# Attention's blocks counted and paced over the slabs, the product operands formed in the last slab, and two of W_o's weights in the values' buffers

## The chip, the cores and the metric

The kernel runs on one core of a Trainium2 chip. The metric is the device time of one execution in microseconds (us); lower is better. Five engines run their own instruction streams side by side: TensorE (PE, matrix products and transposes into PSUM), VectorE (DVE), ScalarE (ACT), GpSimd (POOL) and SyncE (SP, which here only issues DMA transfers). They meet through semaphores: an instruction waits at the head of its engine's stream until its operands are there and its output buffer is free, and all that stands behind it on that engine waits too.

## The reference

The program computes a two-layer trunk on 512 tokens of width 1024. Layer 0 has a convolution module, layer 1 differential attention; each layer ends with a SwiGLU feed-forward part and a gated per-layer embedding. The change lies in layer 1:

```python
def diff_attention(x, w_qkv, ..., lambda_init):          # x: (1, 512, 1024), 8 heads
    q, k, v = jnp.split(x @ w_qkv, 3, axis=-1)
    q = rms_norm(q.reshape(B, S, N_HEADS, 2, HEAD_DIM), q_g) * (HEAD_DIM ** -0.5)
    k = rms_norm(k.reshape(B, S, N_HEADS, 2, HEAD_DIM), k_g)
    ...
    logits = einsum('bhcqd,bhckd->bhcqk', q_blk, k) + bias   # causal, two score maps c
    probs = softmax(where(dist >= 0, logits, -inf))
    w = probs[:, :, 0] - lam * probs[:, :, 1]
    o = rms_norm(einsum('bhqk,bhkd->bhqd', w, v), sub_g) * (1.0 - lambda_init)
    return o.reshape(B, S, N_HEADS * V_DIM) @ w_o

u = rms_norm(h, attn_norm_g); h = h + diff_attention(u, ...)
h = h + swiglu(rms_norm(h, ffn_norm_g), ...)
gate = sigmoid(rms_norm(h, ple_norm_g) @ ple_w_gate)
h = h + gate * (p @ ple_w_proj)
```

## The kernel before, in words

**Exact products from parts.** Every operand of a large product is held as a high part (rounded to the type that PE multiplies fast) and a low part (the rest). `mm3` (L154) makes one product from three matmuls, L156 to L158, each 128x512. A weight is formed by `weight` (L137): SP loads 128x1024 numbers into a buffer "wraw" (two of them) at L145, ACT casts them to the high part "whi" at L149, and DVE, or POOL where `eng=G`, subtracts to get the low part "wlo" at L151. "whi" and "wlo" have four buffers each.

**Six slabs.** Layer 1's attention takes 8 heads in four pairs. The table `QKV` (L80) names six slabs of the projection in order: q 0, v 0, q 1, q 2, v 1, q 3. A "q" slab gives the queries and keys of a pair of heads, a "v" slab the values of four heads. `slab` forms four weights, and for each of four token blocks (tb) `tokens` issues 24 matmuls L156 to L158 into a PSUM accumulator "mm". The values go to buffers B0 to B7 (`values`, L740/L741). A q block goes through `unit` (ACT L757/L760, DVE reduce L764, POOL power L237 and scaling L767) and then `unit_end`: PE transposes it (L773), ACT writes the scaled halves (L781/L782), POOL doubles one (L786), and DVE makes the other parts (L789/L791), all into the C buffers of that pair.

**Heads in blocks.** Attention itself is 32 blocks, 8 heads by 4 query blocks; block (3,2) is head 3, query block 2. Each has three stages. `stage_s` S: scores on PE (L818/L819) into PSUM "sc" (two buffers), added to the bias and evicted by DVE with a running minimum (L821), exponential on ACT (L825), combined on DVE (L828 to L830). `stage_t` T: transposes (L838), split on ACT (L840) and DVE (L841). `stage_a` A: weights times values (L854/L855), collected at L861/L862; after a head's fourth block its norm follows (L866 to L876). `stage_o`: transposes L883 and a split (L180/L181) give the operand of W_o. Block n's step is S(n), T(n-2), A(n-3): 96 stages in all.

**Pace.** The stages are put between the eight chunks of each token block's product: the third entry of a row of `QKV` says how many triples of stages `take` hands to each of the four token blocks. Before, that is 21 triples (63 stages) in the slabs. The others run in `step` calls between later products: the 8 `project` products of layer 1's features with ple_w_proj (three `step` calls each), and then the W_o product, where `heads_until` runs steps until a head's operand is there. `pfeatures` (L270) forms the features' parts (load L273, cast L274, low part L275).

**W_o.** `linear` forms a weight for each of eight outputs m and multiplies it by the eight heads; the first two outputs go together, so that each head's operand serves both as it comes. `add_attn` (L951) adds the result to h on DVE.

**What sets the order.** The Python order is not the engines' order: a scheduler in the framework takes these calls and decides each engine's static instruction order and the waits. The order rows under "The change" show what it decided.

Of the kernel before, what the change touches and what calls it, by code (L numbers as in the profile page):

```python
# [13 lines left out]
F32R = mybir.dt.float32r  # L14
AF = mybir.ActivationFunctionType
ALU = mybir.AluOpType
# [4 lines left out]
P = 128  # L21
S = 512
D = 1024
NC = D // P
NH = 8
# [49 lines left out]
LA = 3  # L75
# [1 line left out]
PACK = True  # L77
E1 = True
GLO = 1
QKV = (("q", 0, (0, 0, 0, 0)), ("v", 0, (0, 1, 1, 0)), ("q", 1, (1, 1, 2, 2)), ("q", 2, (0, 1, 2, 0)), ("v", 1, (1, 2, 2, 2)), ("q", 3, (0, 2, 0, 1)))  # L80


@with_exitstack
def trunk(ctx, tc, xT, pT, wts, diag, dww, vec, rel, onehot, lamv, out):
    nc = tc.nc
    V, A, G, T = nc.vector, nc.scalar, nc.gpsimd, nc.tensor
# [7 lines left out]
    def sb(shape, tag, bufs, dt=F32):  # L94
        uid[0] += 1
        return pool.tile(shape, dt, tag=tag, name=f"{tag}_{uid[0]}", bufs=bufs)
# [10 lines left out]
    f = lambda ap: ap.bitcast(F32)  # L107
# [16 lines left out]
    t = wk()[:, 0:P]  # L124
# [4 lines left out]
    t = tp()  # L129
# [4 lines left out]
    wnext = [0]  # L134
    loaded = [None]

    def weight(n=1024, pieces=1, between=(), eng=V, after=(None, None), home=None):  # L137
        i = wnext[0]
        wnext[0] += 1
        raw = sb([P, 1024], *(home or ("wraw", 2)))  # L140
        hi = sb([P, 1024], "whi", 4, F32R)
        lo = sb([P, 1024], "wlo", 4, F32R)
        for k in range(pieces):
            cut = slice(k * n // pieces, (k + 1) * n // pieces)
            loaded[0] = nc.sync.dma_start(raw[:, cut], wts[i, :, cut])  # L145
            if k < len(between):
                between[k]()
            with tc.issue_after(after[1].ins) if after[1] else nullcontext():
                A.copy(hi[:, cut], raw[:, cut])  # L149
            with tc.issue_after(after[0].ins) if after[0] else nullcontext():  # L150
                eng.tensor_tensor(lo[:, cut], raw[:, cut], f(hi[:, cut]), ALU.subtract)  # L151
        return hi, lo
# [7 lines left out]
    def wpart(w, k):  # L160
        return tuple(t[:, k * P : (k + 1) * P] for t in w)

    def both(t):
        return t[:, 0], t[:, 1]
# [105 lines left out]
    def pfeatures(layer, parts):  # L270
        for k, (hi, lo) in enumerate(parts):
            raw = sb([P, 1024], "wraw", 2)[:, :S]
            nc.sync.dma_start(raw, pT[layer, :, k * S : (k + 1) * S])  # L273
            A.copy(hi, raw)  # L274
            (G if layer == 0 else V).tensor_tensor(lo, raw, f(hi), ALU.subtract)  # L275
        return parts

    last_product = [None]
# [1 line left out]
    def project(ph, m, w, o, step=lambda: None):  # L280

        acc = mm()
        for k in range(2):
            last_product[0] = mm3(acc, wpart(w, 2 * (m % 4) + k), ph[k], k == 0, k == 1)
            step()
        last_copy[0] = A.copy(o, acc)
        return o
# [173 lines left out]
    for c in range(NC):  # L461
# [12 lines left out]
        if c == 1:  # L474
            ph = pfeatures(0, [(sb([P, S], t, 2, F32R), sb([P, S], t, 2, F32R)) for t in ("wth", "wtl")])
# [34 lines left out]
    pp = []  # L510
    pw = [weight(), weight()]
# [55 lines left out]
    with tc.manual_schedule(engines={V.engine, A.engine}):  # L567
        for c in range(NC + 2):
            if c < NC:
# [3 lines left out]
                hi = A.copy(z[c][0], y[c])  # L573
            if c >= 2:
                lo = V.tensor_tensor(z[c - 2][1], y[c - 2], f(z[c - 2][0]), ALU.subtract)
# [2 lines left out]
            if c == 3:  # L578
                third = lo, hi

    def linear(n_in, src, consume, group0=1, before=None, after=None, split={}, home=None):


        m = 0
        while m < NC:
            g = group0 if m == 0 else 1
            ws = [weight(n_in * P, after=split.get(m + i, (None, None)), home=home if m + i == 2 else None) for i in range(g)]
            accs = [mm() for _ in range(g)]
            for k in range(n_in):
                if before:  # L590
                    before(k)
                for w_, a_ in zip(ws, accs):
                    mm3(a_, wpart(w_, k), src[k], k == 0, k == n_in - 1)
                    if after:
                        after()
            for i in range(g):
                consume(m + i, accs[i])
            m += g
# [84 lines left out]
    for k in range(2):  # L683
        t = tp()
# [62 lines left out]
    def unit(pair, ws, tb, between):  # L747

        if tb == 0:
            qk[pair] = [sb([P, 2, S], f"C{i}", 2, F32R) for i in range(6)]  # L750

            for c in range(2):
                with tc.issue_after(n2.last.ins):
                    G.memset(f(qk[pair][4 + c][HALVES[1 - c]]), 0.0)
        acc, r = tokens(ws, tb, between)
        q = big()
        A.activation(q, acc, AF.Copy, scale=r)  # L757
        sq = wk()
        if SQ_ACT:
            A.activation(sq, acc, AF.Square, scale=r)  # L760
        else:
            G.tensor_tensor(sq, q, q, ALU.mult)
        ss = sb([P, P // 2], "v8", 2)[:, :8]
        V.tensor_reduce(out=ss, in_=sq.rearrange("p (g d) -> p g d", g=8), op=ALU.add, axis=AX.X)  # L764
        rs = rsqrt_cols(ss, 8, 1.0 / DH)
        q3 = q.rearrange("p (g d) -> p g d", g=8)
        G.tensor_tensor(q3, q3, rs.unsqueeze(2).to_broadcast([P, 8, DH]), ALU.mult)  # L767
        return pair, tb, q
# [109 lines left out]
    ot = {}  # L878
# [12 lines left out]
    stages = []  # L891
# [2 lines left out]
            if 0 <= at < len(todo):  # L894
                stages.append((n, partial(stage, *todo[at])))

    def take(n):
        got, stages[:n] = [s for _, s in stages[:n]], []
        return got

    waiting = None
    for what, at, pace in QKV:
        ws = slab(GLO if at > 0 else 0)
        for tb in range(4):
            between = take(3 * pace[tb])
            between += [None] * (6 - len(between))
            if waiting:
                between.append(partial(unit_end, *waiting))
                waiting = None
            if what == "v":  # L910
                values(at, ws, tb, between)
            else:
                waiting = unit(at, ws, tb, between)
    unit_end(*waiting)


    done = [0]

    def step():
        if stages:  # L920
            n, s = stages.pop(0)
            s()
        else:
            n = 99
        while done[0] < NH and (n - LA - 3) // 4 > done[0]:
            stage_o(done[0])
            done[0] += 1

    ph = pfeatures(1, [both(sb([P, 2, S], t, 2, F32R)) for t in ("C0", "C1")])
    pp = []  # L930
    for m in range(NC):
        if m % 4 == 0:
            w = weight()
        step()
        if m < 2:
            o = sb([P, S], f"D{m + 2}", 1)
        elif m % 2 == 0:
            o2 = sb([P, 2, S], f"C{m // 2 + 1}", 2)
            o = o2[:, 0]
        else:  # L940
            o = o2[:, 1]
        pp.append(project(ph, m, w, o, step))

    def heads_until(k):
        while done[0] <= k:
# [4 lines left out]
    def add_attn(m, acc):  # L950
        V.tensor_tensor(h[m], acc, h[m], ALU.add)  # L951
        norm.chunk(m)

    linear(NC, ot, add_attn, 2, heads_until, step)
    n2 = Norm("ple_g1")
    ffn(norm, n2)

# [32 lines left out]
def _layout(a):  # L990
# [25 lines left out]
    qkv = a["attn_w_qkv"][0]  # L1016
    for what, at, _ in QKV:
        if what == "v":
# [70 lines left out]
```

## Time and profile before

| what | value |
|---|---|
| median of 3 runs | 1295.92 us (1295.68 to 1297.31) |
| the profiled execution's own time | 1293.82 us |
| its span in the profile | 1292.0 us |
| mean granted TensorE clock | 0.995 |
| last slab matmul starts at | 785.12 us of the span |
| DMA over the span | 131.98 MB, mean 102 GB/s |

All times below are microseconds from the start of the profiled span. In a timeline row the columns are start, duration, engine, line, operation, output <- input, shapes, count, and in brackets the idle time before it and what ended it. Most matmuls overlap: the pitch, from start to start, is what one costs, and not its duration. The page's slices of the span show DVE's load rising in the attention layer (slices 20 to 26), where PE dips to 7 and 8:

```profile
PE   9999999999999999999999997989999999999998
DVE  4897866543344334457678988845443344334445
```

### The profile page before, as it was taken

To read this page: it belongs to the slowest core of one execution; us is meant where nothing else is said; L and a number is where in the kernel's file an instruction comes from. 1 tells how busy PE (TensorE), PEld (TensorE's weight loads), DVE (VectorE), ACT (ScalarE), POOL (GpSimd) and SP (SyncE) were. 2 spreads that over 40 slices of the span, in tenths; PEclk is the share of its full clock that TensorE was granted. 3 is DMA by queue.
4 is the path that set the end of the run, shared out by engine and by line. 5 is a ranking of instruction groups with operands and counts; after the bars stand their busy time and mean duration, and the time that the engine had idled before them with its cause. 6 is when DMAs were issued, how large, how long until landed. Compare 5 with 4: busy or idle time off the path is not lost.

```text
span 1292.0 us, 15534 instructions
## 1 busy us (share of the span) xinstructions
PE 1269.5 (98%) x5960; PEld 1053.6 (82%) x5960; DVE 736.9 (57%) x1143; ACT 521.6 (40%) x826; POOL 236.8 (18%) x199
## 2 busy tenths in 40 slices
PE   9999999999999999999999997989999999999998
PEld 8888788888888888888888886878888888888887
DVE  4897866543344334457678988845443344334445
ACT  5742554332222223345566766634222233222332
POOL 1753432000000000042526534121000000000020
PEclk9999999999999999999999998999999999999999
DMA  7555223333333322233222223123333333332231
GB/s 273 192 177 181 80 76 104 98 98 98 98 98 99 97 86 95 82 117 98 88 90 74 74 66 83 57 76 103 99 98 94 89 97 96 98 98 90 90 115 66
DMA packets 46839, 131.98 MB, mean 102 GB/s; under 512 B 5379, under 2 KB 9987, under 8 KB 46764
## 3 DMA queue, kind: packets, MB, share of 16 engines
q1 hardware_dynamic: 44640, 127.55, 31.0%
q10 hardware_dynamic: 2124, 3.43, 1.0%
q8 instruction: 47, 0.77, 0.2%
q14 instruction: 28, 0.23, 0.1%
HBM read 126.75 MB, written 4.21 MB: 101 GB/s over the span
## 4 chain that ended last, share of the span: by engine, by line
PE 88%; DVE 6%; DMA 3%; issue 2%; ACT 1%; POOL 0%; SPq 0%; DVEq 0%; POOLq 0%; ACTq 0%
PE mm L156 28%; PE mm L157 27%; PE mm L158 27%; DVE sc L419 2%; DVE wlo L151 1%; PE tp L173 1%; PE mm L854 1%; DMA wraw<-in_wts 1%; DMA po<-big 1%; PE sc L818 1%; PE sc L368 1%; PE sc L819 1%; PE tp L838 1%; PE tp L773 0%; DMA h<-in_xT 0%
## 5 line engine op out<-in xcount | busy, mean ns | idle before, releaser
L149 ACT CAST whi<-wraw 128x1024 fp32r<-128x1024 f32 (+2 forms) x213 | 217.6, 1026 | 554.6 <-PE mm L158 364.1
L156 PE MATMUL mm<-A,wlo 128*128 128x512 f32 (+1 forms) x1096 | 427.9, 390 | 4.5 <-DVE wlo L151 3.0
L157 PE MATMUL mm<-A,whi 128*128 128x512 f32 (+1 forms) x1096 | 425.7, 389 | 0.0
L158 PE MATMUL mm<-A,whi 128*128 128x512 f32 (+1 forms) x1096 | 421.8, 389 | 0.0
L151 DVE TENSOR_TENSOR wlo<-wraw,whi 128x1024 fp32r<-128x1024 f32 (+2 forms) x209 | 259.4, 1245 | 84.8 <-ACT whi L149 84.7
L156 PEld LDWEIGHTS mm<-A,wlo 128*128 128x128 f32 x1096 | 206.0, 188 | 48.5 <-DVE wlo L151 3.5
L157 PEld LDWEIGHTS mm<-A,whi 128*128 128x128 f32 x1096 | 206.0, 188 | 42.8 <-issue 1.2
L158 PEld LDWEIGHTS mm<-A,whi 128*128 128x128 f32 x1096 | 205.4, 188 | 42.3 <-issue 0.5
L204 POOL TENSOR_TENSOR acc<-acc,wk 128x512 f32<-128x512 f32 x35 | 58.2, 1662 | 772.3 <-issue 660.1
L156 PE MATMUL mm<-B,wlo 128*128 128x512 f32 x352 | 137.8, 391 | 0.0
L157 PE MATMUL mm<-B,whi 128*128 128x512 f32 x352 | 137.4, 390 | 0.0
L158 PE MATMUL mm<-B,whi 128*128 128x512 f32 x352 | 137.4, 390 | 0.0
L635 DVE TENSOR_TENSOR h<-mm,h 128x512 f32<-128x512 f32 x48 | 33.0, 691 | 122.6 <-PE mm L158 122.5
L627 DVE TENSOR_TENSOR big<-mm,rb 128x512 f32<-128x512 f32 x44 | 30.4, 691 | 126.4 <-PE mm L158 126.4
L625 DVE TENSOR_TENSOR big<-mm,rb 128x512 f32<-128x512 f32 x44 | 30.4, 691 | 99.8 <-PE mm L158 93.0
L158 PEld LDWEIGHTS mm<-B,whi 128*128 128x128 f32 x352 | 66.1, 188 | 14.6
L157 PEld LDWEIGHTS mm<-B,whi 128*128 128x128 f32 x352 | 66.1, 188 | 14.3
L156 PEld LDWEIGHTS mm<-B,wlo 128*128 128x128 f32 x352 | 66.0, 188 | 14.2
L156 PE MATMUL mm<-whi,A 128*128 128x512 f32 x192 | 75.9, 396 | 0.0
L157 PE MATMUL mm<-whi,A 128*128 128x512 f32 x192 | 75.5, 393 | 0.0
L158 PE MATMUL mm<-wlo,A 128*128 128x512 f32 x192 | 74.7, 396 | 0.0
L237 POOL TENSOR_TENSOR r<-v,mhalf 128x8 f32<-128x8 f32 (+1 forms) x31 | 45.8, 1477 | 144.3 <-DVE v L235 135.8
(203 smaller groups left out, 1397.4 us busy)
## 6 DMA issues: line engine op xcount, KB each, us to landing
wraw<-in_wts SPq DMA_DIRECT2D x193, 512.0 KB, 3.5
wraw<-in_wts SPq DMA_DIRECT2D x16, 384.0 KB, 3.0
D<-in_diag SPq DMA_DIRECT2D x22, 256.0 KB, 4.3
C<-in_diag SPq DMA_DIRECT2D x16, 256.0 KB, 4.8
h<-in_xT SPq DMA_DIRECT2D x8, 256.0 KB, 5.4
bias<-scr ACTq DMA_DIRECT2D x8, 256.0 KB, 3.5
out_t<-h SPq DMA_DIRECT2D x7, 256.0 KB, 2.0
wraw<-in_wts SPq DMA_DIRECT2D x4, 256.0 KB, 5.0
```

What stands on the lines that cost most here:

```text
L149: A.copy(hi[:, cut], raw[:, cut])
L151: eng.tensor_tensor(lo[:, cut], raw[:, cut], f(hi[:, cut]), ALU.subtract)
L156: T.matmul(acc, al, bh, start=first, stop=False)
L157: T.matmul(acc, ah, bh, start=False, stop=False)
L158: return T.matmul(acc, ah, bl, start=False, stop=last)
L173: r = T.matmul(t[:, cut], src[:, cut], ones, start=first and b == 0, stop=last and b == 3)
L204: self.last = self.eng.tensor_tensor(self.acc, self.acc, sq, ALU.add)
L237: last_pow[0] = G.tensor_tensor(r[:, :n], v[:, :n], mhalf[:, :n], ALU.pow)
L419: last_v_tap[0] = V.scalar_tensor_tensor(sum_, tap(j), wt(c, j), sum_, ALU.mult, ALU.add)
L625: V.tensor_tensor(tg, pg, rb, ALU.mult)
L627: V.tensor_tensor(tu, pu, rb, ALU.mult)
L635: V.tensor_tensor(h[m], acc, h[m], ALU.add)
```

## The change

1. The table `QKV` paces whole blocks rather than triples of stages: `take` counts blocks, and hands out all stages of the blocks counted so far. There are 26 blocks (73 stages) in the slabs; v 0 gets 6, q 1 four, q 2 six, v 1 five, q 3 five.
2. Layer 1's features (`pfeatures`) are formed within the last slab, after its second token block, in B0 and B1, which held values of the first four heads. Their low parts are made by POOL, and no longer by DVE.
3. ple_w_proj's two weights are formed there too: the first after the third token block in B2/B3, with its low part on POOL, the second after the fourth in C0/C1, with its low part on DVE.
4. The eight products have all their outputs in C2 to C5, one `step` stands before and one after each (16 instead of 24), and `step` issues at most one `stage_o`.
5. W_o's fifth and sixth weights (m = 4, 5) have their parts in B0/B1 and B2/B3 instead of the "whi"/"wlo" buffers.

```diff
-QKV = (("q", 0, (0, 0, 0, 0)), ("v", 0, (0, 1, 1, 0)), ("q", 1, (1, 1, 2, 2)), ("q", 2, (0, 1, 2, 0)), ("v", 1, (1, 2, 2, 2)), ("q", 3, (0, 2, 0, 1)))
+QKV = (("q", 0, (0, 0, 0, 0)), ("v", 0, (1, 1, 2, 2)), ("q", 1, (1, 1, 1, 1)), ("q", 2, (1, 1, 2, 2)), ("v", 1, (1, 1, 2, 1)), ("q", 3, (1, 1, 1, 2)))
...
-    def weight(n=1024, pieces=1, between=(), eng=V, after=(None, None), home=None):
+    def weight(n=1024, pieces=1, between=(), eng=V, after=(None, None), home=None, parts=None, bufs=1):
...
-        hi = sb([P, 1024], "whi", 4, F32R)
-        lo = sb([P, 1024], "wlo", 4, F32R)
+        hi = sb([P, 1024], *((parts[0], bufs) if parts else ("whi", 4)), F32R)
+        lo = sb([P, 1024], *((parts[1], bufs) if parts else ("wlo", 4)), F32R)
...
-            (G if layer == 0 else V).tensor_tensor(lo, raw, f(hi), ALU.subtract)
+            G.tensor_tensor(lo, raw, f(hi), ALU.subtract)
...
-    def take(n):
-        got, stages[:n] = [s for _, s in stages[:n]], []
+    taken = [0]
+
+    def take(blocks):
+
+        taken[0] += blocks
+        got = [s for n, s in stages if n < taken[0]]
+        del stages[: len(got)]
         return got
...
-            between = take(3 * pace[tb])
+            between = take(pace[tb])
...
+            if (what, at, tb) == ("q", 3, 1):
+                ph = pfeatures(1, [both(sb([P, 2, S], t, 1, F32R)) for t in ("B0", "B1")])
+            elif (what, at, tb) == ("q", 3, 2):
+                pw = [weight(eng=G, parts=("B2", "B3"))]
+            elif (what, at, tb) == ("q", 3, 3):
+                pw.append(weight(parts=("C0", "C1"), bufs=2))
     unit_end(*waiting)
...
-        while done[0] < NH and (n - LA - 3) // 4 > done[0]:
+        if done[0] < NH and (n - LA - 3) // 4 > done[0]:
             stage_o(done[0])
             done[0] += 1
 
-    ph = pfeatures(1, [both(sb([P, 2, S], t, 2, F32R)) for t in ("C0", "C1")])
     pp = []
     for m in range(NC):
-        if m % 4 == 0:
-            w = weight()
+        if m % 2 == 0:
+            o2 = sb([P, 2, S], f"C{m // 2 + 2}", 2)
         step()
-        if m < 2:
-            o = sb([P, S], f"D{m + 2}", 1)
-        elif m % 2 == 0:
-            o2 = sb([P, 2, S], f"C{m // 2 + 1}", 2)
-            o = o2[:, 0]
-        else:
-            o = o2[:, 1]
-        pp.append(project(ph, m, w, o, step))
+        pp.append(project(ph, m, pw[m // 4], o2[:, m % 2]))
+        step()
...
-    linear(NC, ot, add_attn, 2, heads_until, step)
+    linear(NC, ot, add_attn, 2, heads_until, step, parts={4: ("B0", "B1"), 5: ("B2", "B3")})
```

`linear` passes `parts.get(m + i)` on to `weight`. Since the file grows, lines behind L893 stand three to five further down in the changed program (L951 becomes L956).

The first place is PE's order in the third Q slab (q 2), where head 2's last score block meets head 3's. "sc" are score accumulators, "tp" transposes, "mm" with "whi"/"wlo" token products, "mm" with "B" the products with values. Before:

```order
L818 MATMUL sc_5626<-C_898_5011,C_896_5009 128x128
L819 MATMUL sc_5626<-C_900_5013,C_896_5009 128x128
L156 MATMUL mm_5758<-whi_5735,A_731_4229 128x512
L157 MATMUL mm_5758<-whi_5735,A_730_4228 128x512
L854 MATMUL mm_5617<-B_855_4824,wth_5610 128x256
L838 MATMUL tp_5643<-ident_65,big_5496 128x128 x3
L773 MATMUL tp_5654<-ident_65,big_5547 128x128 x4
L855 MATMUL mm_5617<-B_855_4824,wtl_5611 128x128
L854 MATMUL mm_5617<-B_869_4898,wth_5610 128x256
L855 MATMUL mm_5617<-B_869_4898,wtl_5611 128x128
L818 MATMUL sc_5772<-C_898_5011,C_896_5009 128x256
L819 MATMUL sc_5772<-C_900_5013,C_896_5009 128x256
```

And in the changed program, at the same heads:

```order
L818 MATMUL sc_5541<-C_916_5077,C_914_5075 128x512
L819 MATMUL sc_5541<-C_918_5079,C_914_5075 128x512
L818 MATMUL sc_5614<-C_915_5076,C_913_5074 128x128
L819 MATMUL sc_5614<-C_917_5078,C_913_5074 128x128
L773 MATMUL tp_5578<-ident_65,big_5520 128x128 x4
L838 MATMUL tp_5631<-ident_65,big_5442 128x128 x3
L818 MATMUL sc_5652<-C_915_5076,C_913_5074 128x256
L819 MATMUL sc_5652<-C_917_5078,C_913_5074 128x256
L818 MATMUL sc_5614<-C_916_5077,C_914_5075 128x128
L819 MATMUL sc_5614<-C_918_5079,C_914_5075 128x128
L818 MATMUL sc_5652<-C_916_5077,C_914_5075 128x256
L819 MATMUL sc_5652<-C_918_5079,C_914_5075 128x256
```

The token matmuls that stood between score products have moved away from this place (before, six of them stand between the two 128x512 products of block (2,3) and twelve more behind the second); now the score products follow each other, and further rows of blocks (2,2), (2,3) and (3,2) stand on both sides without a token matmul.

The second place is ACT's order behind the last slab. "C" with "tp" are the halves written by `unit_end`, "whi" W_o's high parts. Before:

```order
L781 ACTIVATE C_1152_6145<-tp_6399,lam_4521 64x2x128
L782 ACTIVATE C_1154_6147<-tp_6399,vec_63 64x2x128
L781 ACTIVATE C_1153_6146<-tp_6399,lam_4521 64x2x128
L782 ACTIVATE C_1155_6148<-tp_6399,vec_63 64x2x128
L825 ACTIVATE big_6527,st_6201<-big_6527,st_6201 128x512
L866 ACTIVATE wk_6469<-D_1174_6234 128x512
L825 ACTIVATE rb_6533,st_6201<-rb_6533,st_6201 128x512
L692 DMA bias_6739<-scr 128x512
L825 ACTIVATE big_6564,st_6560<-big_6564,st_6560 128x128
L149 CAST whi_6454<-wraw_6453 128x1024
L825 ACTIVATE acc_6569,st_6560<-acc_6569,st_6560 128x128
L149 CAST whi_6672<-wraw_6671 128x1024
```

In the changed program:

```order
L757 ACTIVATE big_6425<-mm_6360,rcol_4585 128x512
L760 ACTIVATE wk_6427<-mm_6360,rcol_4585 128x512
L149 CAST C_1246_6556<-wraw_6555 128x1024
L149 CAST whi_6897<-wraw_6896 128x1024
L781 ACTIVATE C_1162_6180<-tp_6407,lam_4521 64x2x128
L782 ACTIVATE C_1164_6182<-tp_6407,vec_63 64x2x128
L781 ACTIVATE C_1163_6181<-tp_6407,lam_4521 64x2x128
L782 ACTIVATE C_1165_6183<-tp_6407,vec_63 64x2x128
```

Before, the two casts of ple_w_proj (whi_6454, whi_6672) stand behind the `unit_end` set shown and behind exponentials. Now the cast of ple_w_proj's second weight (into C_1246) and that of W_o's second weight (whi_6897) stand ahead of that set and of two more that follow.

The third place is DVE's order around the fifth weight of W_o, at the end of the four products that wait for head 7. Before:

```order
L181 SCALAR_TENSOR_TENSOR A_1362_7015<-tp_7009,lam_4521,A_1361_7014 128x512
L951 TENSOR_TENSOR h_7_86<-mm_6864,h_7_86 128x512
L951 TENSOR_TENSOR h_8_87<-mm_6865,h_8_87 128x512
L951 TENSOR_TENSOR h_9_88<-mm_7057,h_9_88 128x512
L951 TENSOR_TENSOR h_10_89<-mm_7096,h_10_89 128x512
L151 TENSOR_TENSOR wlo_7131<-wraw_7129,whi_7130 128x1024
L151 TENSOR_TENSOR wlo_7170<-wraw_7168,whi_7169 128x1024
```

In the changed program:

```order
L181 SCALAR_TENSOR_TENSOR A_1361_7008<-tp_7002,lam_4521,A_1360_7007 128x512
L956 TENSOR_TENSOR h_7_86<-mm_6902,h_7_86 128x512
L956 TENSOR_TENSOR h_8_87<-mm_6903,h_8_87 128x512
L956 TENSOR_TENSOR h_9_88<-mm_7056,h_9_88 128x512
L956 TENSOR_TENSOR h_10_89<-mm_7095,h_10_89 128x512
L151 TENSOR_TENSOR wlo_7208<-wraw_7206,whi_7207 128x1024
L151 TENSOR_TENSOR wlo_7247<-wraw_7245,whi_7246 128x1024
```

The low parts of the fifth and sixth weights (wlo_7131 and wlo_7170 before) no longer stand behind the four additions; in their place stand those of the seventh and eighth.

More of the change, by code (lines that the diff above doesn't have):

```diff
@@ L579, in trunk, with linear @@
                 third = lo, hi
-    def linear(n_in, src, consume, group0=1, before=None, after=None, split={}, home=None):
+    def linear(n_in, src, consume, group0=1, before=None, after=None, split={}, home=None, parts={}):
         m = 0
@@ L586, in linear @@
             g = group0 if m == 0 else 1
-            ws = [weight(n_in * P, after=split.get(m + i, (None, None)), home=home if m + i == 2 else None) for i in range(g)]
+            ws = [weight(n_in * P, after=split.get(m + i, (None, None)), home=home if m + i == 2 else None, parts=parts.get(m + i)) for i in range(g)]
             accs = [mm() for _ in range(g)]
```

## The prediction

> **What bounds the kernel now.** I read the page's table of engines first, then the share of the clock and the busy time in windows, then TensorE's waits, and last the timeline at each wait that the edit can reach.
>
> ```profile
> span 1292.0 us, 15534 instructions
> PE 1269.5 (98%) x5960; PEld 1053.6 (82%) x5960; DVE 736.9 (57%) x1143; ACT 521.6 (40%) x826; POOL 236.8 (18%) x199
> ```
>
> TensorE (PE) is busy for 98% of the span, so a change that alters no matmul can win only where PE stands still. Both programs issue the same matmuls. The place is the attention layer, and there the windows say more than the page's averages (columns: PE, PEld, DVE, ACT, POOL busy us, then granted clock, DMA share, GB/s).
>
> ```profile
> 660.00:680.00 20.00, 20.00 (x104) 16.85 (x104) 15.61 (x42) 11.54 (x28) 4.71 (x4) 1.00 0.34 120
> 740.00:760.00 20.00, 18.62 (x104) 15.61 (x103) 17.85 (x49) 14.63 (x34) 7.14 (x7) 1.00 0.20 67
> 790.00:800.00 10.00, 4.39 (x15) 3.60 (x16) 7.81 (x24) 5.92 (x14) 4.66 (x5) 0.60 0.57 134
> 800.00:810.00 10.00, 8.13 (x38) 6.09 (x37) 9.62 (x25) 8.10 (x18) 1.91 (x3) 0.89 0.63 193
> 850.00:860.00 10.00, 6.19 (x28) 4.61 (x27) 6.53 (x7) 4.77 (x7) 2.58 (x2) 1.00 0.09 15
> ```
>
> VectorE (DVE) has 17.85 us of work in 20 us inside the slabs, so it has next to no slack there: 57% over the span hides this. Right behind the slabs PE is busy for 4.39 of 10 us, at a clock of 0.60, and around 855 it stands again. TensorE's waits between 620 and 900 name the reasons (us in total, times, longest).
>
> ```profile
> PE sc L818 <- DVE st L821: 5.7, 6, 1.4
> PE mm L156 <- DVE wlo L151: 4.7, 2, 3.0
> PE sc L818 <- DVE v L871: 2.7, 1, 2.7
> PE mm L156 <- ACT A L180: 0.8, 1, 0.8
> ```
>
> The first and third are a score product (L818) that finds both PSUM buffers "sc" still held until DVE has evicted them (L821). The second is a weight whose low part is late. All of these sum to 14 us, about 1% of the span: that is everything a rearrangement here can win or multiply.
>
> **The change, part by part.** The sum is made against the profiled execution's own 1293.82 us; the median of the runs shown is 1295.92, which is 2.1 higher, and I carry the sum over to it.
>
> *Work moved into the slabs: +1.9, and as much less behind them.* By the PE order, 24 score pairs of 128x512 columns instead of 20 and 51 pairs L854/L855 instead of 46 stand between the first and the last slab matmul. (Each score group has two such matmuls, which makes two groups more.) The pitch comes from the timeline:
>
> ```profile
> 774.64 0.39 PE L158 MATMUL mm<-wlo,A 128*128 128x512 f32 x1
> 774.87 0.39 PE L156 MATMUL mm<-whi,A 128*128 128x512 f32 x1
> 785.12 0.39 PE L158 MATMUL mm<-wlo,A 128*128 128x512 f32 x1
> ```
>
> It is 0.23 us for 512 columns, so two groups of two are 0.9 us; five pairs of 256 and 128 columns are 5 x 384/512 x 0.23 = 0.9 us; one transpose more is some 0.1. The last row is the last slab matmul; I count from it. So of the ten stages that the new table adds inside the slabs (73 planned against 63) only one score block arrives there: the old order held nearly as many.
>
> *The crowd in the third Q slab: +4.5 (1.4 to 6).* Four blocks' score products now follow each other with no token matmul between. PE's own rows from the second half of block (2,2) to the first of (3,2) are some 7,400 columns, 14.5 x 0.23 = 3.3 us, and 0.5 for the short transposes: about 4 us. DVE must in the same stretch run what stands in its order, and its groups between 640 and 860 give the price (busy us, mean ns of one).
>
> ```profile
> L789 DVE SCALAR_TENSOR_TENSOR C<-tp,lam,C 64x256 fp32r<-64x256 f32 x32 | 15.5, 484 | 3.5 <-ACT C L782 2.0 <-PE sc L819 0.8
> L764 DVE TENSOR_REDUCE v<-wk 128x8 f32<-128x512 f32 x12 | 8.2, 683 | 5.4 <-ACT wk L760 5.1
> L821 DVE CUSTOM_DVE_ANT_0 big<-sc,bias 128x512 f32<-128x512 f32 x8 | 5.5, 683 | 0.9 <-PE sc L819 0.9
> L821 DVE CUSTOM_DVE_ANT_0 acc<-sc,bias 128x384 f32<-128x384 f32 x8 | 4.4, 548 | 2.2 <-PE sc L819 2.2
> L841 DVE TENSOR_TENSOR wtl<-tp,wth 128x256 fp32r<-128x256 f32 x8 | 3.4, 419 | 0.9 <-ACT wth L840 0.8
> L821 DVE CUSTOM_DVE_ANT_0 big<-sc,bias 128x256 f32<-128x256 f32 x8 | 3.3, 417 | 0.1
> L821 DVE CUSTOM_DVE_ANT_0 big<-sc,bias 128x128 f32<-128x128 f32 x8 | 2.3, 283 | 1.8 <-PE sc L819 1.8
> L275 DVE TENSOR_TENSOR C<-wraw,C 128x512 fp32r<-128x512 f32 x2 | 1.6, 777 | 0.0
> ```
>
> Evictions: 2 x 0.55 + 2 x 0.68 + 0.42 + 2 x 0.28 = 3.4; four halves L789/L791 at 0.48 make 1.9; two reduces L764 1.4; L841 0.4; L862 as much; L830 for 384 columns 0.6; a dozen small ones at 0.08 to 0.26 the other 1.5: 9.6 us. Consecutive records overlap (a 0.69 us operation is followed after 0.62), so DVE needs some 8.4. PE has 4; the difference, 4.4 and a little for the hand-over, is the stop. It is 1.4 if DVE enters the stretch idle, since then only the chain from the transposes L773 through L781/L782 to L789/L791 counts (four ACT pieces of 0.47, two DVE of 0.48, less what PE does meanwhile); 6 if DVE enters it late. The row I lean on is the 17.85 of 20: DVE doesn't come idle. The next rows are L830's price, and two waits of before, where the same evictions lie among token matmuls and single short waits remain:
>
> ```profile
> 786.21 0.62 DVE L830 SCALAR_TENSOR_TENSOR big<-acc,st,big 128x384 f32<-128x384 f32 x1
> 754.00 0.41 PE L818 MATMUL sc<-C,C 128*128 128x384 f32 x1 [1.38 <-DVE st L821]
> 724.10 0.33 PE L818 MATMUL sc<-C,C 128*128 128x128 f32 x1 [0.67 <-DVE st L821]
> ```
>
> *Other places in the slabs: +1.3 (0 to 1.5) and -1.2 (-2.5 to 0).* In the second V slab block (4,3) stands right behind the transposes it needs: the same chain, 1.3 us, with nothing between. Of the two waits just quoted (2.1 us, 2.5 with the slow start behind each) I take half as gone, because the blocks there are spread differently.
>
> *Between the last slab matmul and head 7's transposes L883: 0 (-5.2 to +3).* Three timeline rows belong to it:
>
> ```profile
> 788.47 0.30 PE L818 MATMUL sc<-C,C 128*128 128x128 f32 x1 [0.57 <-ACT C L274]
> 788.21 0.47 ACT L781 ACTIVATE C<-tp,lam 64x256 fp32r<-64x256 f32 x1
> 850.48 0.60 PE L883 MATMUL tp<-ident,D 128*128 128x128 f32 x4
> ```
>
> Before, this takes 850.48 - 785.12 = 65.4 us for 50.9 us of PE work by pitch. After, the work is 48.9. The features and the first product weight are formed earlier, so the 0.57 us wait behind L274 and the two low parts L275 (1.6 us of DVE) leave. But something takes the place: ScalarE (ACT) now has the cast of W_o's second weight directly behind that of the second product weight, ahead of the three L781/L782 sets of the last Q slab. That load can only be issued when the product weight's low part has freed a raw buffer, and SP's queue sends the next weight's load with it. Before's chain has exactly such a pair, and the DMA view of 640 to 780 a lone load:
>
> ```profile
> 790.07 6.28 DMA wraw<-in_wts
> 796.38 1.05 ACT whi L149
> wraw<-in_wts SPq DMA_DIRECT2D x16, 512.0 KB, 3.7
> ```
>
> From the last slab matmul: cast done at +1.0, low part 1.25 (the L151 row, further down), load 6.3, cast 1.05, then L781 to L791 and the transposes' first user, block (6,1), at +12.3. PE has 3.2 us of other work and so stops for 9. Then DVE's rows up to block (7,3) sum to 31 us, 27 with the overlap: (7,3) at +39.7, and 25 us of PE work remain: +65. The low end is the 3.7 load (2.6 less) and DVE a tenth quicker; the high end a DVE that also waits for POOL. I take 0: one stop is exchanged for its like.
>
> [...]
>
> *W_o's fifth and sixth weights: -2.9 (-2.2 to -3.0).* Before, they wait for buffers "whi"/"wlo" that the first four hold until the last L158 of a pair.
>
> ```profile
> 853.80 1.07 PE L158 MATMUL mm<-A,whi 128*128 128x512 f32 x4
> 854.23 2.48 DVE L951 TENSOR_TENSOR h<-mm,h 128x512 f32<-128x512 f32 x4 [1.64 <-PE mm L158]
> 854.23 1.99 ACT L149 CAST whi<-wraw 128x1024 fp32r<-128x1024 f32 x2 [2.42 <-PE mm L158]
> 857.90 0.50 PE L156 MATMUL mm<-A,wlo 128*128 128x512 f32 x1 [3.03 <-DVE wlo L151]
> L151 DVE TENSOR_TENSOR wlo<-wraw,whi 128x1024 fp32r<-128x1024 f32 x22 | 31.7, 1446 | 4.7 <-ACT whi L149 4.7
> ```
>
> PE ends its four closing products at 854.87, and the low part starts only behind four L951. With both weights formed in the values' buffers PE needs only a PSUM accumulator, which the first L951 frees (854.23 + 0.7 = 854.9): 857.90 becomes some 855. Its cover: the buffers come free when the last L854/L855 have read the values, and the forming takes 1.05 + 1.25 plus a load that is already there; PE has over 10 us of products meanwhile. The seventh weight then has two products' time, 2 x 5.5 = 11 us. Without the cover the term is 0. This part is the surest.
>
> **Sum:** 1.9 + 4.5 + 1.3 - 1.2 - 0 - 2.9 = +3.6 us. (The 1.9 is not taken off again behind the slabs, because that stretch is set by the load and by DVE.) Own time 1293.8 becomes 1297.4; on the median's scale 1299.5.
>
> **The rivals.** *Faster, 1291.2:* DVE enters the third Q slab with slack and the load travels alone. Then 1.9 + 1.4 + 0 - 2.5 - 2.6 - 2.9 = -4.7. For it: DVE had 15.61 of 20 us at 660 to 680, and the two L275 are gone. Against it: the second L145 is next in SP's queue and has its buffer.
>
> *No change, 1295.7:* only the chain counts in the crowd and the rest is as forecast: 1.9 + 1.4 + 0.6 - 1.2 - 0 - 2.9 = -0.2. This is also what remains if the edit doesn't do what it says: with one score block moved instead of ten stages there is little to gain or lose but the tail.
>
> *Slower yet, 1302.6:* the low parts that go from DVE to POOL hold DVE up.
>
> ```profile
> 749.37 1.81 DVE L829 SCALAR_TENSOR_TENSOR st<-st,lam 128x1 f32<-128x1 f32 x1
> 748.77 2.40 POOL L151 TENSOR_TENSOR wlo<-wraw,whi 128x1024 fp32r<-128x1024 f32 x1 [2.30 <-ACT whi L149]
> 785.95 0.22 DVE L829 SCALAR_TENSOR_TENSOR st<-st,lam 128x1 f32<-128x1 f32 x1
> ```
>
> The same one-column operation takes 1.81 us while POOL forms a low part and 0.22 without: 1.6 us lost. The change puts one whole low part and two of half the width on POOL in the last slab: up to 1.6 + 2 x 0.8 = 3.2 us of DVE, paid by PE where DVE is the bound, less the 0.1 that fits in gaps: +6.7. It decides from the point at which DVE's order has no slack of that size between those operations and the next eviction. For it: 17.85 of 20. Against it: DVE is relieved of 1.6 us of L275 and 1.25 of L151 by the same move, so that the net is near 0.
>
> [...]
>
> **How the numbers follow.** Forecast 0.31, the faster rival 0.28, no change 0.25, slower yet 0.14; 0.02 lie elsewhere. About 0.2%, 2.6 us, is what a measurement of this kernel can tell from no change. The forecast at +3.6 is beyond that by 1 us only, and the crowd's price alone decides between it and no change. So faster 0.29, same 0.27, slower 0.44. The range goes from the faster rival's 1291 to 1304, just above the slower one's; the likeliest case alone would have 1298 to 1302. The extremes of every bound at once (-7.4 and +10.2) are left outside.
>
> **What would show it.** In the third Q slab PE should wait 3 us or more at the score products of blocks (3,0) to (3,2), on L821: if those waits sum to under 1.5, the crowd was misjudged and the time is at most 1296. Behind the last slab matmul one stop of 8 to 10 us with a released cast L149 on a load of over 6 us; if it is 6 or less, the load was alone. From there to head 7's L883 it should be 65 us; the W_o products should run on through the fourth-to-fifth weight with under 0.5 us of wait. [...] The forecast is wrong outright if DVE is idle for over 3 us of every 20 in the last three slabs.

## The result, and the profile after

The changed kernel takes 1310.01 us (median of 4 runs, 1305.97 to 1310.49), the kernel before 1296.62 us in the same comparison: a ratio of 1.0097, 95% interval 1.0075 to 1.0118. By the ratio it is slower by some 12.5 us. The forecast was 1299.5, +3.6, with a range to 1304: the sign was right, the size more than three times too small.

The page of the changed kernel begins as follows; its profiled execution took 1310.49 us, against 1293.82 before, 16.7 more.

```profile
span 1308.7 us, 15538 instructions
PE 1281.9 (98%) x5960; PEld 1059.6 (81%) x5960; DVE 735.4 (56%) x1140; ACT 524.7 (40%) x826; POOL 246.9 (19%) x202
```

The same number of matmuls, 98% again, and 12 us more of "busy" on PE: part of the loss is hidden in matmuls that ran longer. Three timeline rows of PE divide the loss: the last slab matmul, head 7's transposes, and the weight load with which W_o's fifth output begins (PEld is PE's weight load, beside the matmul).

```profile
806.13 0.39 PE L158 MATMUL mm<-wlo,A 128*128 128x512 f32 x1
870.13 0.60 PE L883 MATMUL tp<-ident,D 128*128 128x128 f32 x4
874.65 0.19 PEld L156 LDWEIGHTS mm<-A,B 128*128 128x128 f32 x1 [0.52 <-DVE h L956]
```

| stretch (us, by matmul starts) | before | after | difference | forecast |
|---|---|---|---|---|
| first to last slab matmul | 172.95 | 194.41 | +21.5 | +6.5 |
| last slab matmul to head 7's last transpose | 65.7 | 64.3 | -1.4 | 0 |
| from there to PE's last matmul | 436.5 | 433.6 | -2.9 | -2.9 |

The slabs hold all of the error. PE's waits between 600 and 900 have a releaser at their head that is absent from before's list:

```profile
PE mm L854 <- ACT wth L840: 9.0, 9, 2.0
PE sc L818 <- DVE C L789: 3.3, 2, 1.8
...
PE sc L818 <- DVE st L821: 1.0, 4, 0.4
```

The values product (L854) waits nine times for ScalarE's copy of its block's transposed weights (L840); seven of the nine, 7.4 us, lie in the slabs. The windows show the third Q slab and the second V slab (busy us of PE, PEld, DVE, ACT, POOL, then granted clock, DMA share, GB/s):

```profile
720.00:740.00 20.00, 16.72 (x67) 12.94 (x67) 16.82 (x47) 13.69 (x34) 12.17 (x12) 0.74 0.06 14
740.00:760.00 20.00, 19.09 (x108) 16.19 (x107) 19.02 (x56) 15.36 (x38) 9.67 (x11) 1.00 0.37 119
```

PE's clock is 0.74 in a place where it was 1.00 before, and only 67 PE instructions start in 20 us. One of those waits, from both sides, PE's rows and then ACT's:

```profile
720.51 0.60 PE L773 MATMUL tp<-ident,big 128*128 128x128 f32 x4
...
721.36 0.39 PE L838 MATMUL tp<-ident,big 128*128 128x128 f32 x2
723.35 0.39 PE L854 MATMUL mm<-B,wth 128*128 128x256 f32 x1 [1.61 <-ACT wth L840]
```

```profile
721.23 0.45 ACT L781 ACTIVATE C<-tp,lam 64x256 fp32r<-64x256 f32 x1
721.59 0.46 ACT L782 ACTIVATE C<-tp,vec 64x256 fp32r<-64x256 f32 x1
722.07 0.47 ACT L781 ACTIVATE C<-tp,lam 64x256 fp32r<-64x256 f32 x1
722.44 0.46 ACT L782 ACTIVATE C<-tp,vec 64x256 fp32r<-64x256 f32 x1
722.92 0.37 ACT L840 CAST wth<-tp 128x256 fp32r<-128x256 f32 x1
```

PE transposes a Q block (L773) and the weights of block (2,1) (L838), and its next instruction is block (2,1)'s values product. ACT serves in order: four pieces of the Q block first, 1.7 us, then the copy. PE stands for 1.6 us. Before, 4.4 us of other PE work lay between the same two instructions.

That spacing can be counted in the order itself: PE work, at full-speed pitch, between a block's last transpose and its first values product. Before, 3 of the first 21 blocks have under 2 us; after, 10 have. I call such a place **bunched**, and one where a score buffer is needed again within 3.5 us of work likewise.

Of the four executions of experiment 1's kernel the first, the profiled one, took 3311 us, against 1315 to 1321 in the other three.

### The profile page after: what moved, and what is told of

It is laid out like the page before. It is cut to its first block, busy times and chain, and to the rows that moved or that the text cites. A ratio compares the mean times of both kernels' runs of the same rounds, so it can differ in the third digit from the quotient of the medians.

```text
span 1308.7 us, 15538 instructions
## 1 busy us (share of the span) xinstructions
PE 1281.9 (98%) x5960; PEld 1059.6 (81%) x5960; DVE 735.4 (56%) x1140; ACT 524.7 (40%) x826; POOL 246.9 (19%) x202
## 4 chain that ended last, share of the span: by engine, by line
PE 91%; DVE 3%; ACT 2%; DMA 2%; issue 1%; SPq 0%; POOL 0%; ACTq 0%; DVEq 0%; POOLq 0%
PE mm L156 28%; PE mm L157 28%; PE mm L158 28%; PE sc L368 2%; PE tp L173 1%; PE mm L854 1%; DMA wraw<-in_wts 1%; PE mm L368 1%; PE mm L324 1%; DVE wlo L151 1%; ACT C L781 0%; PE sc L818 0%; ACT C L782 0%; PE tp L838 0%; PE sc L819 0%
## 5 line engine op out<-in xcount | busy, mean ns | idle before, releaser
L149 ACT CAST whi<-wraw 128x1024 fp32r<-128x1024 f32 (+2 forms) x209 | 214.0, 1028 | 550.8 <-PE mm L158 353.8
L156 PE MATMUL mm<-A,wlo 128*128 128x512 f32 (+1 forms) x1080 | 421.3, 390 | 2.5 <-ACT A L180 2.0
L157 PE MATMUL mm<-A,whi 128*128 128x512 f32 (+1 forms) x1080 | 419.3, 388 | 0.0
L158 PE MATMUL mm<-A,whi 128*128 128x512 f32 (+1 forms) x1080 | 415.6, 389 | 0.0
L151 DVE TENSOR_TENSOR wlo<-wraw,whi 128x1024 fp32r<-128x1024 f32 (+2 forms) x205 | 254.7, 1246 | 85.9 <-ACT whi L149 85.7
L156 PEld LDWEIGHTS mm<-A,wlo 128*128 128x128 f32 x1080 | 202.8, 188 | 45.4 <-ACT A L180 2.6
L157 PEld LDWEIGHTS mm<-A,whi 128*128 128x128 f32 x1080 | 202.8, 188 | 42.3 <-issue 1.2
L158 PEld LDWEIGHTS mm<-A,whi 128*128 128x128 f32 x1080 | 202.5, 188 | 42.0 <-issue 0.5
```

The costliest lines, as they stand in the source:

```text
L156: T.matmul(acc, al, bh, start=first, stop=False)
L157: T.matmul(acc, ah, bh, start=False, stop=False)
L158: return T.matmul(acc, ah, bl, start=False, stop=last)
```

## The experiments

Theory A: bunching costs. Rival B: operands formed in the last slab, with low parts on POOL. Rival C: more blocks than DVE can take in the slabs. Rival D: the waits come from elsewhere, and adjacency is harmless.

**1. The pace alone** (and the same kernel once more, for its profile). The edit, in the kernel before:

```diff
-QKV = (... ("v", 0, (0, 1, 1, 0)), ("q", 1, (1, 1, 2, 2)), ...)
+QKV = (... ("v", 0, (1, 1, 2, 2)), ("q", 1, (1, 1, 1, 1)), ...)      # the changed table
-            between = take(3 * pace[tb])
+            between = take(pace[tb])                                 # whole blocks, the changed take
```

> The kernel before with the new table and whole-block pace only (features, product weights and W_o's weights as before). Theory A (the pace puts each block's values product right behind its transposes, so that PE waits for ScalarE's copy): the six slabs take 194 us from first to last slab matmul instead of 173, PE waits 8 us or more in all on L840, and the time is 13 to 20 us over the kernel before (1310 to 1317). Rival B (the operands formed in the last slab, with low parts on POOL, cost it): the slabs take at most 180 us and the time is within 7 us of before.

> The kernel of the first experiment again, for an undisturbed profile. Theory A: slabs 190 to 197 us from first to last slab matmul, 8 us or more of PE waits on L840, no gain behind W_o, time 1313 to 1321.

Measured: 1318.41 us, the median of the three (1319.54 with the fourth), where before had 1297.59, ratio 1.0152 (1.0133 to 1.0171); in the second run 1311.12, from one execution. There the slabs take 188.7 us and the stretch behind head 7 437.2, so without its gain. Rival B is out as the main cause: with the old operands the loss is as large. The loss and the missing gain behind head 7 came as theory A had them; several of its numbers were missed by a little: 1310 to 1317 for the first run, and for the second 1313 to 1321, slabs of 190 to 197 and 8 us or more on L840, where 7.9 were measured. Within the slabs the waits on L840 (seven, 6.9 us) stand at the same products as those of the changed kernel, such as

```profile
721.86 0.39 PE L854 MATMUL mm<-B,wth 128*128 128x256 f32 x1 [1.61 <-ACT wth L840]
```

**2. The old pace with all the rest of the change.**

```diff
-            between = take(pace[tb])
+            between = take(3 * pace[tb])          # with the old table and the old take
```

> The changed kernel with the old table and the old triples of stages; operands in the last slab and W_o's weights in values' buffers as changed. Theory A: the slabs are back at 173 to 176 us, the W_o tail keeps its 2.9 us, and the time is 1291 to 1296, at or under the kernel before. Rival B: the last slab and what follows still lose 8 us or more, and the time is 1303 or above.

Measured: 1296.62 against 1297.59, ratio 0.9990 (0.9982 to 0.9999). The slabs take 172.9 us, as before to 0.1; behind head 7 it keeps the 2.9 us, and between it loses 2.4 (68.1 instead of 65.7). So the whole slab loss belongs to the pace; the upper end of A's range was missed by 0.6.

**3. W_o's two weights alone, in the kernel before.**

```diff
-    linear(NC, ot, add_attn, 2, heads_until, step)
+    linear(NC, ot, add_attn, 2, heads_until, step, parts={4: ("B0", "B1"), 5: ("B2", "B3")})
```

> The kernel before with W_o's fifth and sixth weights in B0/B1 and B2/B3, nothing else. If the tail term of the prediction is right, PE's wait of 3.0 us on L151 at the fifth weight goes and the time falls by 2.9 us (2 to 3.2). Rival: the gain after W_o in the changed kernel came from elsewhere (earlier operands), and the time moves by under 1 us.

Measured: 1296.51 against 1297.59, ratio 0.9986 (0.9977 to 0.9996), about -1.8: under the 2 to 3.2 that were expected. PE's one wait left on a weight's low part (that of ple_w_proj's product), and the weight load with which W_o's fifth output now begins:

```profile
PE mm L156 <- DVE wlo L151: 1.5, 1, 1.5
```

```profile
860.07 0.19 PEld L156 LDWEIGHTS mm<-A,B 128*128 128x128 f32 x1 [0.52 <-DVE h L951]
```

Of the two waits on L151 the 3.0 us one is gone, and the stretch behind head 7 is 433.5 instead of 436.5: the term is right in its place. But the stretch ahead of it grew from 65.7 to 69.0. PE's waits there are nearly as before (9.4 us in all, 8.7 before), while the granted clock over that stretch is 0.90 in this profile and 0.92 in before's: 13.7 us at half speed (clock 0.50) instead of 10.2, which is at most 1.7 of the 3.3. Where the rest comes from isn't settled.

**4. The same blocks in the same places, cut elsewhere.** The changed kernel's portions are S, T, A; this one leaves each portion's last values product to the next, so that portions are A, S, T, as the old triples were.

```diff
         got = [s for n, s in stages if n < taken[0]]
+        got = got[: max(0, len(got) - (taken[0] > LA))]
```

> The changed kernel, the same 26 blocks in the same places, but each portion of stages ends ahead of its last values product, which opens the next portion (one stage less at each cut). Theory A: PE's work between transposes and values product is back over 2 us for all but 3 of the first 21 blocks (10 are under 2 in the changed kernel), PE's waits on L840 fall from 9 us to under 3, the slabs take 180 to 186 us and the time is about 1300 (1296 to 1303). Rival C (the number of blocks in the early slabs, DVE and ACT being full, is what costs): the slabs stay over 190 us and the time over 1306.

Measured: 1298.56, ratio 1.0009 (0.9999 to 1.0018): 11 us of the 12.5 are gone with one stage moved at each cut. The slabs take 182.3 us. The waits between 600 and 900:

```profile
PE sc L818 <- DVE st L821: 4.0, 7, 1.3
PE sc L818 <- DVE C L789: 2.6, 1, 2.6
...
PE mm L854 <- ACT wth L840: 0.5, 1, 0.5
```

L840 fell from 9.0 to 0.5. Most of what remains of the slabs' loss sits between 712 and 752, where PE loses 10.4 us over its pitch instead of 2.8 before: among the bunched score products of heads 2 and 3, the place that the prediction priced.

**5. Spread.** Experiment 4's cut, and 24 blocks placed so that nothing is bunched.

```diff
+QKV = (("q", 0, (0, 0, 0, 0)), ("v", 0, (0, 1, 1, 2)), ("q", 1, (1, 1, 1, 2)),
+       ("q", 2, (1, 1, 1, 2)), ("v", 1, (1, 1, 2, 2)), ("q", 3, (1, 1, 1, 1)))
```

> The changed kernel with portions that end ahead of a values product, and 24 blocks spread so that none bunch: v 0 (0,1,1,2), q 1 (1,1,1,2), q 2 (1,1,1,2), v 1 (1,1,2,2), q 3 (1,1,1,1). In PE's order no values product has under 2 us of work behind its transposes in the slabs and no score buffer is needed again within 3.5 us of work. Theory A (bunching costs, not the number of blocks): the slabs take 173 to 177 us with some 2 us more work in them, PE has under 1 us of waits on L840 there, the W_o tail keeps 2.9 us, and the time is 1291.5 to 1295.5, under the kernel before. Rival C (the number of blocks in slabs in which DVE is full): the slabs take 182 us or more, and the time is 1298 or above.

Measured: 1291.95 where before had 1295.92, ratio 0.9963 (0.9949 to 0.9977): **faster than both kernels**. The slabs take 173.8 us with 1.4 us more PE work in them than before's. One window decides against rival C:

```profile
720.00:740.00 20.00, 20.00 (x110) 17.15 (x110) 19.00 (x49) 14.92 (x35) 13.32 (x12) 1.00 0.33 106
```

DVE is busy for 19.00 of 20 us, more than in the changed kernel's same window (16.82), and PE is busy throughout. A nearly full DVE was not by itself a bound here. Nor is the load over the slabs what separates this run from experiment 4: from the first to the last slab matmul, first experiment 4, then this one, DVE (the third busy time) and ACT have nearly the same work, in 182.3 us and in 173.8.

```profile
612.37:794.66 182.29, 178.02 (x894) 148.46 (x893) 139.65 (x354) 117.36 (x257) 85.13 (x79) 0.98 0.26 80
612.65:786.42 173.77, 172.25 (x888) 144.67 (x886) 139.11 (x346) 116.10 (x255) 86.17 (x77) 1.00 0.26 82
```

All 26 blocks in places that do not bunch were not run. Of the 4 us between the medians the profiles place 2.3 (from the first slab matmul to PE's last: 672.8 us against 675.1). The profiled execution of before, at 1293.82 us, is itself 2.1 quicker than the median of before's runs here; that of this kernel, at 1291.96, stands at its median.

**6. The old numbers of blocks in whole blocks.**

```diff
+QKV = (... ("v", 0, (0, 3, 1, 0)), ("q", 1, (1, 1, 2, 2)), ("q", 2, (0, 1, 2, 0)), ...)   # old counts, S, T, A
```

> The changed kernel with the old table's numbers of blocks (v 0 gets 4, q 1 six, q 2 three, v 1 seven, q 3 three), but in whole blocks, so that each portion ends behind a values product. In PE's order 7 of the first 21 blocks have under 2 us of work between transposes and values product, and 8 score buffers are needed again within 3.5 us. Theory A: bunching comes back with the cut alone; the slabs take 180 to 190 us, waits on L840 are 3 us or more, and the time is 1301 to 1308. Rival C: with the old numbers the slabs stay at 173 to 177 us and the time at 1294 to 1298.

Measured: 1304.81 against 1295.92, ratio 1.0056 (1.0036 to 1.0076). The slabs take 181.5 us; what is handed out differs from experiment 2 only by the cut, one stage later each time, and that costs 8.5 us in the slabs. The waits on L840 are only 1.6 us in the slabs (3.0 over the attention layer), so A's "3 us or more there" is missed: here the loss is shared with others, and one wait behind the slabs that no theory had named is the largest.

```profile
PE tp L773 <- POOL big L767: 6.6, 1, 6.6
PE mm L854 <- ACT wth L840: 3.0, 4, 1.6
PE sc L818 <- POOL C L786: 2.0, 1, 2.0
```

**7. The values product one block earlier, in the kernel before.**

```diff
-LA = 3
+LA = 2
```

> The kernel before with one constant changed, the lag of the values product (2 blocks instead of 3), so that it follows its own block's transposes. Old pace, old cuts, operands and weights as before. In PE's order 10 of the first 21 blocks have under 2 us between the two. Theory A: the slabs take 185 to 195 us, PE waits on L840 for 5 us or more, time 1307 to 1318. Rival D (ScalarE's copy is quick enough; the changed kernel's waits came from its features and weights in the last slab or from the early start in v 0): the slabs within 4 us of 173, time under 1301.

Measured: 1331.99 against 1295.92, ratio 1.0271 (1.0249 to 1.0293). The slabs take 193.0 us: with the old table, the old triples and the old operands, moving each values product next to its transposes costs 20 us there, and rival D is out. But this is not the price of the wait for ACT's copy alone. The constant moves every values product, and what follows it, one block ahead; of PE's waits in the slabs only 2.4 us are on L840, 2.8 on L821, and the longest, 3.4, is a token matmul's for a weight's cast (L149). Two numbers were missed. The waits on L840 are 4.1 us in the whole layer and not 5; and the time is 14 us above the expected 1307 to 1318, since another 14 us are lost behind the slabs, mostly in

```profile
PE tp L773 <- POOL big L767: 8.6, 1, 8.6
```

| kernel | bunched of 21 | slabs | to head 7 | behind it | ratio to before |
|---|---|---|---|---|---|
| before | 3 | 172.9 | 65.7 | 436.5 | 1 |
| changed | 10 | 194.4 | 64.3 | 433.6 | 1.0097 |
| 1, pace alone | 10 | 188.7 | 66.9 | 437.2 | 1.0152 |
| 2, old pace | 4 | 172.9 | 68.1 | 433.6 | 0.9990 |
| 3, W_o's weights alone | 3 | 173.0 | 69.0 | 433.5 | 0.9986 |
| 4, cut ahead of A | 3 | 182.3 | 63.6 | 433.5 | 1.0009 |
| 5, spread | 0 | 173.8 | 65.5 | 433.6 | 0.9963 |
| 6, old counts, cut behind A | 6 | 181.5 | 70.4 | 433.5 | 1.0056 |
| 7, LA = 2 | 9 | 193.0 | 79.5 | 439.3 | 1.0271 |

(The slabs and the next two columns are from one profile each, in us; "bunched" counts, in PE's order in the trace, blocks with under 2 us of work between transposes and values product. In the changed kernel an eleventh has 1.99. For experiments 6 and 7 the expectations had counted one more each.)

## Why the prediction was right or wrong

**The tail, -2.9: right,** and its reason too. The first L956 frees the PSUM buffer at 874.6, and PE's weight load waits 0.52, where PE had stood for 3.0; every kernel with the two weights in the values' buffers shows 433.5 or 433.6 behind head 7. Alone, in the kernel before, it gave 1.8 of the 2.9 (experiment 3).

**Between the slabs and head 7, 0: the size was about right (-1.4), by luck, for the mechanism was wrong.** The 9 us stop behind W_o's second weight did not come, since its load did not wait for the second product weight's low part. The changed kernel's timeline (DVE, SP's queue, ACT, PE):

```profile
802.68 1.23 DVE L151 TENSOR_TENSOR wlo<-wraw,whi 128x1024 fp32r<-128x1024 f32 x1 [1.98 <-ACT whi L149]
803.94 0.33 SPq L145 DMA_DIRECT2D wraw<-in_wts  x1
807.36 1.05 ACT L149 CAST whi<-wraw 128x1024 fp32r<-128x1024 f32 x1 [0.35 <-PE tp L773]
807.39 1.22 DVE L151 TENSOR_TENSOR C<-wraw,C 128x1024 fp32r<-128x1024 f32 x1
...
820.95 0.41 PE L818 MATMUL sc<-C,C 128*128 128x384 f32 x1 [1.51 <-DVE C L789]
825.26 0.47 PE L818 MATMUL sc<-C,C 128*128 128x512 f32 x1 [1.79 <-DVE C L789]
```

The product weight's low part (into C) begins at 807.39; W_o's second weight was being cast by then. SP had issued its load at 803.94, when W_o's *first* weight's low part (802.68 + 1.23) freed a raw buffer. I had taken the raw buffers to be used in strict turn, and they were not. The load was in hand 3.4 us later, when its cast began. So the loads didn't travel as a pair, and instead of one long stop there are several of 1 to 2 us, the longest on DVE's halves of the Q blocks. The same stretch takes 63.6 to 70.4 us in the other kernels with the new weights, so that 64.3 was no certain outcome.

**Work moved into the slabs, +1.9: right** (1.7 by the pitches of the records). Its 24 and 20 are single score matmuls, 12 pairs and 10, and not pairs; the 0.9 us was reckoned for four matmuls, so the sum stands.

**The crowd in the third Q slab, +4.5: the place was right, the size short, and the reason mostly another.** In the changed kernel PE starts block (2,2)'s second score product at 720.86 and the values product behind (3,2)'s at 732.31: 11.5 us for the 4 us of PE work that the prediction counted, 7.5 lost. The prediction had named its sign: 3 us or more of waits on L821 at the score products of blocks (3,0) to (3,2), and a misjudged crowd under 1.5. There is one such wait, of 0.37 us. PE stood behind ACT's copy (1.61, shown above, and 0.32) and for short moments behind others, and then ran at half speed:

```profile
724.38 0.50 PE L818 MATMUL sc<-C,C 128*128 128x512 f32 x1 [0.64 <-POOL C L786]
730.56 0.58 PE L818 MATMUL sc<-C,C 128*128 128x256 f32 x1 [0.37 <-DVE st L821]
732.31 0.58 PE L854 MATMUL mm<-B,wth 128*128 128x256 f32 x1 [0.32 <-ACT wth L840]
```

```profile
725.41:735.65 10.24, 9.50 (x30) 7.53 (x31) 9.03 (x30) 7.16 (x19) 4.52 (x5) 0.50 0.12 26
```

So the clock was left out: in that window it is 0.50, and the token products that start at 733.12 and 733.55 lie 0.43 us apart, instead of 0.23, though nothing stops them. Experiment 4 has the same crowd without the bunched values products around it. There the priced mechanism does show, at blocks (3,0) and (3,1), with 1.9 us in all:

```profile
724.43 0.33 PE L818 MATMUL sc<-C,C 128*128 128x128 f32 x1 [1.14 <-DVE st L821]
726.18 0.33 PE L818 MATMUL sc<-C,C 128*128 128x128 f32 x1 [0.63 <-DVE st L821]
```

It loses 7.6 more than before at this place (712 to 752), some 3 of it in slow 128x512 matmuls (granted clock 0.91 from 720 to 760).

**"Other places in the slabs: +1.3 and -1.2" is the step that failed.** I had looked for score buffers and for transposes that a score product needs, in two or three places; the wait of a values product for ACT's copy was not in the list, since before it shows nowhere in the slabs: all but 3 of the first 21 blocks have 2.8 us of work or more between the two. Of the slabs' 21.5 us the moved work takes 1.7 and the crowd 7.5; the other 12.3 stand where these two terms had +0.1 together. The two small terms themselves did little harm: at block (4,3) PE waits 0.1 us, not 1.3, and the waits on L821 in the slabs fall by 1.1 as forecast. PE's waits from the first to the last slab matmul, first of the kernel before (its only entry), then of the changed one:

```profile
PE sc L818 <- DVE st L821: 2.1, 2, 1.4
```

```profile
PE mm L854 <- ACT wth L840: 7.4, 7, 2.0
PE sc L818 <- DVE st L821: 1.0, 4, 0.4
PE sc L818 <- POOL C L786: 0.6, 1, 0.6
PE tp L838 <- DVE big L830: 0.4, 1, 0.4
PE mm L855 <- DVE wtl L841: 0.3, 1, 0.3
```

Besides, 17.1 us of the changed kernel's slabs ran at half speed (from 667.38, 725.41 and 769.78; none before), which costs up to 8.5 us. Most of this comes from the cut: before, a triple ended with T, and the next one began with A; whole blocks end with A. Experiments 4 and 6 move nothing but that, and it is worth 12.1 and 8.5 us of the slabs. The 9.3 us that experiment 4 still loses there go with the new table's places for the blocks, since experiment 5, with other places and nearly the same work, loses 0.8. Why the framework's scheduler turns a cut one stage later into transposes and values product side by side was not taken apart.

**The rivals.** "Slower yet" had the right side for a reason that the runs don't bear out: pace alone, without the low parts moved to POOL, is as slow. In the last two token blocks one DVE operation of four columns takes over 1 us beside POOL, against 0.14 to 0.17 where POOL forms no low part (one of 2.15, at 775.47, stands beside a slab weight's low part, which POOL forms in both kernels):

```profile
794.23 2.40 POOL L151 TENSOR_TENSOR B<-wraw,B 128x1024 fp32r<-128x1024 f32 x1
795.43 1.22 DVE L871 TENSOR_TENSOR v<-v,r 128x4 f32<-128x4 f32 x1
```

It ends with POOL's low part (796.65 and 796.63), as the 1.81 us operation did in the kernel before (751.18 and 751.17), and costs 1 us, not 3: such operations were rarer than that rival assumed. "No change" and "faster" assumed a DVE with slack; in experiment 5 PE ran on beside a nearly full DVE (19.00 of 20 us) where the distances were kept.

## What to carry to other kernels

When a change re-makes an order, list for each producer and consumer pair on the bound engine how much of its work lies between the two, before and after, for all pairs and all places. A pair whose distance falls below the other engine's chain (here the copy, behind four pieces of another chain) can become a wait, whatever the busy shares say; the kernel before has three such pairs in the slabs without one. Where a pace hands out portions of a pipeline, try where the portion ends: here portions that end with the transposes cost 12.1 and 8.5 us less than the same ones that end with a values product.

## What the runs showed of the hardware

The clock fell from 1.00 to 0.50 without a long stop. The changed kernel and the pace alone have the same PE order up to 799.5 us, 6.6 us ahead of the last slab matmul, and the same waits but for one that is 0.6 us longer; 3.4 us windows around 667, first of the changed kernel, then of the pace alone (which runs 0.1 us later):

```profile
663.97:667.38 3.41, 2.20 (x11) 1.71 (x12) 3.01 (x15) 3.22 (x8) 0.00 (x0) 1.00 0.85 249
667.38:670.79 3.41, 3.41 (x10) 2.68 (x9) 2.45 (x5) 2.66 (x8) 0.00 (x0) 0.50 0.32 85
```

```profile
663.90:667.30 3.40, 2.15 (x13) 1.54 (x12) 3.00 (x15) 3.05 (x8) 0.00 (x0) 1.00 0.82 267
667.30:670.70 3.40, 3.40 (x18) 2.86 (x17) 3.40 (x11) 3.12 (x9) 0.00 (x0) 1.00 0.17 50
```

In the first, PE was busy for 2.20 of 3.41 us, with no single wait over 0.61, and then ran 3.41 us at half speed: 10 matmuls instead of 18, 1.6 us lost. In the second, nearly the same, 2.15 of 3.40, cost nothing. Over the slabs this makes 194.4 against 188.7 us, in three steps of about 1.6 and that one wait.

The traces suggest why the first lost and the second did not. Between 600 and 900 us the stretches at half speed of every profile but the 3311 us one last 3.41 us or a whole multiple, and within a profile they lie on one grid of that step. In the changed kernel the grid has a line at 667.38; in the pace alone, whose clock next falls at 723.49, it has lines at 662.05, 665.46 and 668.88. The pauses that fall into one window of the grid in the first (shown above) are shared by two in the second, with PE busy for 2.92 and 2.67 us, over 69% of each:

```profile
662.05:665.46 3.41, 2.92 (x15) 2.03 (x14) 3.14 (x8) 1.21 (x3) 0.00 (x0) 1.00 0.67 215
665.46:668.88 3.42, 2.67 (x14) 2.24 (x14) 3.29 (x12) 3.42 (x11) 0.00 (x0) 1.00 0.57 171
```

Over these nine profiles, from 600 to 900 us, a full-speed window of the grid was always followed by half speed where PE was busy for under 43% of it (13 windows), never where it was busy for over 69%, and in 15 of 35 cases between. What decides between these two shares isn't shown. In the changed kernel's slabs scattered short waits thus cost up to nearly twice their sum: some 10 us of waits, and up to 8.5 for the clock. The same pauses just ahead of 667 cost 1.6 us in one profile and nothing in the other. The changed kernel's own runs may spread for this reason: the slowest, 1310.49 us, had a mean granted clock of 0.991, the fastest, 1305.97, of 0.995. More than that was not shown for them.
